# GELU moved from the state space groups to the gate, and a second set of attention buffers, in a one-layer hybrid encoder step

## The chip, the cores and the metric

One core of one Trainium2 chip runs the whole step. The metric is the device time of one execution in microseconds (us), as the median of several runs. Engines are named as the profile names them: PE is TensorE's matmul side and PEld its weight loads, DVE is VectorE, ACT is ScalarE, POOL is GpSimd, SP is SyncE, which issues the DMAs.

## The reference

One layer is computed for 2048 prompt positions and 32 sample positions, width 1024, everything in float32:

```python
h = rmsnorm(x, ln1_g) * (1 + sc1) + sh1
q, k, v, u = split(h @ w_in)                        # 8 heads, 2 kv heads, 32 groups of 16 channels
attn = sink_attention(rope(norm(q)), rope(norm(k)), v)   # own chunk of 64 and the 128 before it
ssm_y, h_last = s5(u, ...)                          # scan over positions, 64 complex states a group
g = gelu(ssm_y)
ssm_o = g * sigmoid(g @ ssm_glu_w + ssm_glu_b)
merged = concat(rmsnorm(attn), rmsnorm(ssm_o))
x = x + g1 * (merged @ w_out)
h2 = rmsnorm(x, ln2_g) * (1 + sc2) + sh2
x = x + g2 * ((silu(h2 @ w_gate) * (h2 @ w_up)) @ w_down)
```

GELU is taken element by element, so it may be applied where `ssm_y` is made or anywhere between there and its first use in `g @ ssm_glu_w` and `g * sigmoid(...)`.

## The kernel before

Tokens are handled in 17 tiles: 16 of 128 prompt positions and one of the 32 sample positions. They are taken in the order of `TILES`, prompt tiles 8 to 15, then 0 to 7, then the sample tile. "The k-th tile" below counts in that order from 0, so the 8th is prompt tile 0. Every float32 product is made of three matmuls of a high and a low half (`mm3`, L117), and nearly every operand is first split in two: ACT rounds the high half, DVE or POOL subtracts to get the low half (L101, L89).

There are four stages, all in one function:

- Stage A (to about 355 us): modulation vectors, input projection, matrices of the state space layer. The q, k, v columns of prompt tiles 0 to 5 are put off (`LATE`).
- Stage B (about 355 to 555 us): the 32 state space groups (`ssm_group`, L950), the projections put off (`deferred`, L841), and the first attention tiles (`attention_tile`, L1097). A group transposes its inputs, makes two products `v1` and `v2`, scans them on DVE, adds up `y` in PSUM, and ACT writes `t` from it with GELU (L992). `t` goes to DRAM (`gt_d`).
- Stage C (about 555 to 960 us): the remaining attention tiles, the gate (`c_prep`, L1288), the norms (`c_norm`, L1335) and the output projection (`c_out`, L1366). `c_prep` takes units of 256 tokens in the order 4, 5, 6, 7, 0, 1, 2, 3 and the sample as unit 8. Two units share one loaded buffer `gr` of 512 tokens (`g_load`, L1273): it is loaded by four DMAs when the second unit of the pair before is done, and there is only one such buffer. A unit splits `gr` into `gh` and `gl`, multiplies by `glh` and `gll` (the GLU weights) into `cb`, takes a Tanh on ACT (L1321) and multiplies by `gr` on DVE.
- Stage F (from about 962 us): gate, up and down projections, PE-bound, with SiLU on ACT.

An attention tile splits q, k and v, transposes them, and then has two halves of queries `o` = 0 and 1. For each half it makes scores `s` (8 matmuls) and calls `softmax` (L1046): DVE takes maxima into `st`, ACT takes four Exp from `s` into the buffer `pbuf` of that half with running sums, DVE finishes the sums, POOL scales `pbuf`. Then `p_split` (L1063) transposes `pbuf` on PE into `pt` and splits that into `th` and `tl`, and `p_values` (L1076) multiplies with the values into `ob` and copies to `att`. There is one `pbuf` for each half, shared by all tiles:

```python
    pe_ = [pb_.tile([128, 4, 256], F32, name=f"pbuf{o}") for o in range(2)]
```

The flows are Python generators that a class `Flow` steps in turn; attention runs as

```python
    fa = Flow(attention_tile, NT, 2, 5)
```

at most 2 tiles at a time, a new one when the last has made 5 steps, and at most `NATT` = 6 tiles ahead of the output projection. What order the instructions of one engine finally have is decided by a scheduler when the kernel is built (L1897), so a change in one flow moves instructions of the others too. Within an engine the order is then fixed: an instruction whose input is late holds up all that stand behind it.

Between stages B and C the weights `glh`, `gll` (`glu_steps`, L1180) and the eight `woh`, `wol` of the output projection (`wo_steps`, L1167) are loaded and split. The pool that holds the GLU weights and the first four `woh` is opened when the one of the projections put off (`qin`, L1199) is closed.

Of the kernel before, what the change touches and what calls it, by code (L numbers as in the profile page):

```python
# [10 lines left out]
F32 = mybir.dt.float32  # L11
F32R = mybir.dt.float32r
I32 = mybir.dt.int32
AF = mybir.ActivationFunctionType
# [9 lines left out]
NT = NPT + 1  # L24
# [13 lines left out]
NSC = DEC // LC  # L38
# [35 lines left out]
def hybrid_kernel(  # L74
# [10 lines left out]
    V, A, P, PE, SP = nc.vector, nc.scalar, nc.gpsimd, nc.tensor, nc.sync  # L85
# [14 lines left out]
    def act(out, a, func=AF.Copy, **kw):  # L100
        A.activation(out, a, func, **kw)  # L101

    def f(a):
        return a.bitcast(F32)
# [811 lines left out]
    pb_ = bin_.enter_context(tc.tile_pool(name="pb", bufs=1, reuse_waits="tile", side="right"))  # L916
# [30 lines left out]
    def part(t, dt=F32R):  # L947
        return pss.tile([128, XC], dt, tag=t, name=t)

    def ssm_group(g):  # L950
        b_, gi_ = divmod(g, GB)
        us, uss = bt_[b_]
        sm = pss.tile([128, SM], F32R, tag="sm", name="sm", bufs=SMB)
        SP.dma_start(f(sm), sm_d[g])
        ec = pss.tile([128, 2, XC], F32, tag="ec", name="ec", bufs=SMB)
        for h in range(2):
            SP.dma_start(ec[64 * h:64 * h + 64], e_d[g])
        Th, Tl = sm[:, 0:128], sm[:, 128:256]
        M1, M2 = f(sm[:, 256:384]), f(sm[:, 384:512])
        up = mbank([128, XC], nm="up")  # L960
        yield 1
        for b in range(2):
            PE.transpose(up[:, 128 * b:128 * b + 128], us[:, b, gi_].rearrange("c l h -> c (l h)"), ident)
        PE.transpose(up[:, 256:262], uss[:, gi_].rearrange("c l h -> c (l h)"), ident[0:6, 0:6])
        uh, ul = part("uh"), part("ul")
        split(uh, ul, up, A, V)
        yield 1
        v1 = mbank([128, XC], nm="v1", tag="v1", bufs=1)
        v2 = mbank([128, XC], nm="v2", tag="v2", bufs=1)
        mm3(v1, sm[:, 512:640], sm[:, 704:832], uh, ul, True, True)  # L970
        mm3(v2, sm[:, 576:704], sm[:, 768:896], uh, ul, True, True)
        w = part("w", F32)
        t = part("t", F32)
        tt(V, w[:, 1:XC], v1[:, 0:XC - 1], ec[:, 0, 1:XC], MULT)
        tt(V, t[:, 1:XC], v2[:, 0:XC - 1], ec[:, 1, 1:XC], MULT)
        tt(P, w[:, 1:XC], w[:, 1:XC], t[:, 1:XC], ADD)
        P.tensor_copy(w[:, 0:258:257], zh[:, g])
        V.tensor_tensor_scan(w[:, 1:257], r8[:, g:g + 1].to_broadcast([128, 256]), w[:, 1:257], 0.0, op0=MULT, op1=ADD)
        V.tensor_tensor_scan(w[:, 258:262], r8[:, g:g + 1].to_broadcast([128, 4]), w[:, 258:262],
                             zh[:, g, 1:2], op0=MULT, op1=ADD)  # L980
        yield 1
        for i, (e, xf) in enumerate(((P, xf1), (P if g % 2 else V, xf2))):
            x = w if i else t
            tt(e, x, w, ec[:, i], MULT)
            P.tensor_copy(xf[:, :, g], x[:, 256:262:5])
        yield 1
        y = mbank([128, XC], nm="y", tag="y", bufs=YB)
        mm3(y, Th, Tl, uh, ul, True, False)
        mm(y, M1, t, False, False)
        mm(y, M2, w, False, True)  # L990
        g2 = t
        act(g2, y, AF.Gelu_apprx_tanh)  # L992
        yield 1
        SP.dma_start(gt_d[16 * g:16 * g + 16].rearrange("h l c -> l h c"), g2[:, 0:256])
        P.tensor_copy(gsm[:, :, g], g2[:, 257:261])
        yield 1
# [26 lines left out]
    ts(V, nsink, nsink, -1.0)  # L1023
    ts(V, nsinks, nsinks, -1.0)

    pe_ = [pb_.tile([128, 4, 256], F32, name=f"pbuf{o}") for o in range(2)]
    P.memset(pe_[0][:, :, 192:256], 0.0)
    P.memset(pe_[1][:, :, 0:64], 0.0)

    def kv_split(kf, vf, dst, n):  # L1030

# [63 lines left out]
    atts = {}  # L1095

    def attention_tile(j):  # L1097
        j = TILES[j]
        n = 128 if j < NPT else DEC
        qkv = pb2.tile([128, QKV], F32, tag="qkv", name="qkv", bufs=1)  # L1100
        SP.dma_start(qkv[0:n], qkv_d[j * 128:j * 128 + n])
        yield 1
        qs = pb2.tile([128, NH, 128], F32R, tag="qs", name="qs", bufs=1)
        qv = qkv[0:n, 0:512].rearrange("p (h d) -> p h d", d=HD)
        split(qs[0:n, :, 0:64], qs[0:n, :, 64:128], qv, A, P)
        qt = pb2.tile([128, NH * 128], F32R, tag="qt", name="qt", bufs=1)
        qw = n // 2 if j < NPT else n
        qtv = qt[:, 0:NH * n].rearrange("p (o h q) -> p h o q", h=NH, q=qw)
        for hb in range(2):
            qb = bbank([128, 4, 128], F32R, nm="qb")  # L1110
            for i in range(4):
                PE.transpose(qb[:, i, 0:n], qs[0:n, hb * 4 + i], identr[0:n, 0:n])
            cp(V if hb else A, qtv[:, hb * 4:hb * 4 + 4], f(qb[:, :, 0:n]).rearrange("p h (o q) -> p h o q", q=qw))
        kf = qkv[0:n, 512:640].rearrange("p (h d) -> p h d", d=HD)
        vf = qkv[0:n, 640:768].rearrange("p (h d) -> p h d", d=HD)
        kt = pb2.tile([128, 4, 256], F32R, tag="kt", name="kt")
        att = pat.tile([128, 4, 128], F32, tag="att", name="att", bufs=NATT)
        atts[j] = att
        if j < NPT:
            vcur = kv_split(kf, vf, kt[:, :, 128:256], n)  # L1120
            if j == TILES[0]:
                pkv = pb2.tile([128, 2, 128], F32, tag="ckv", name="pkv", bufs=1)
                SP.dma_start(pkv, qkv_d[(j - 1) * 128:j * 128, 512:768].rearrange("t (a d) -> t a d", a=2))
                vprev[0] = kv_split(pkv[:, 0].rearrange("p (h d) -> p h d", d=HD),
                                    pkv[:, 1].rearrange("p (h d) -> p h d", d=HD), kt[:, :, 0:128], 128)
            elif j:
                V.tensor_copy(kt[:, :, 0:128], f(vprev[1][:, :, 128:256]))
            vpt = [vprev[0], vcur]
            vprev[0], vprev[1] = vcur, kt
            yield 1  # L1130
            vlist = [(vpt[0], 128), (vcur, 128)]
            kbs = (0, 1) if j else (1,)
            for o in range(2):
                lo, hi = (64 * o, 192 + 64 * o) if j else (128, 192 + 64 * o)
                sp = [bbank([128, 2, 256], nm="s") for _ in range(2)]
                for pr in range(4):
                    for x in range(2):
                        mm(sp[pr // 2][:, pr % 2, lo:hi], qt[:, 512 * o + 128 * pr:512 * o + 128 * pr + 128],
                           kt[:, (pr // 2) * 2 + x, lo:hi], x == 0, x == 1)
                softmax(sp, pe_[o], lo, hi, nsink)  # L1140
                yield 1
            for o in range(2):
                parts = []
                for kv in range(2):
                    parts.append(p_split(pe_[o], kbs, 2, kv))
                    yield 1
                p_values(parts, vlist, kbs, 2, att[:, :, 64 * o:64 * o + 64])
        else:
            ckv = pb2.tile([128, 2, 128], F32, tag="ckv", name="ckv", bufs=1)
            SP.dma_start(ckv[:, 0], cache_k[0, 0].rearrange("t h d -> t (h d)"))  # L1150
            SP.dma_start(ckv[:, 1], cache_v[0, 0].rearrange("t h d -> t (h d)"))
            vc = kv_split(ckv[:, 0].rearrange("p (h d) -> p h d", d=HD), ckv[:, 1].rearrange("p (h d) -> p h d", d=HD),
                          kt[:, :, 0:128], 128)
            vo = kv_split(kf, vf, kt[:, :, 128:160], n)
            sp = bbank([128, 2, 256], nm="s")
            for kv in range(2):
                for x in range(2):
                    mm(sp[:, kv, 0:160], qt[:, 128 * kv:128 * kv + 128], kt[:, kv * 2 + x, 0:160], x == 0, x == 1)
            P.memset(pe_[0][:, 0:2, 160:192], 0.0)
            softmax([sp], pe_[0], 0, 160, nsinks)  # L1160
            yield 1
            parts = [p_split(pe_[0], (0, 1), 1, kv) for kv in range(2)]
            yield 1
            p_values(parts, [(vc, 128), (vo, DEC)], (0, 1), 1, att[:, :, 0:DEC])
        yield 1
# [23 lines left out]
    def stage(nm):  # L1189
        return pw1.tile([128, 512], F32, tag="tc", name=nm, bufs=TC)  # L1190

    fa = Flow(attention_tile, NT, 2, 5)
    n = 0
    while fd.next < fd.n or fd.live:
        for fl, st, lim in ((fm, FM, G), (fd, FDS, G), (fa, FAS, NATT)):
# [75 lines left out]
    graw, ssm = {}, {}  # L1271
# [16 lines left out]
    def c_prep(u):  # L1288

        u = UNITS[u]  # L1290
        b, h = divmod(u, 2)
        if u == UNITS[0]:
            g_load(b)
        n = 256 if u < 8 else DEC
        nch = n // LC
        g = graw[b][:, :, :, nch * h:nch * h + nch].rearrange("p k l c -> p k c l")
# [14 lines left out]
        for i in range(2):  # L1311
# [3 lines left out]
            for m in range(2):  # L1315
                o = 256 * i + 128 * m
# [495 lines left out]
    for n, (L, u, p) in enumerate(steps):  # L1812
# [19 lines left out]
        b = PRODUCTS[p][2]  # L1832
# [68 lines left out]
```

## Time and profile before

| what | value |
|---|---|
| median of 3 runs | 2361.86 us (2360.06 to 2366.63) |
| profiled execution, its own time | 2357.34 us |
| its span, first to last instruction | 2355.6 us |
| mean granted clock of PE | 0.967 |
| PE, PEld busy | 94%, 87% of the span |
| DVE, POOL, ACT busy | 76%, 56%, 53% |
| DMA queue of the kernel | 52.8% of 16 engines' span |

The span is the time from the first to the last instruction on the core, and the busy time of an engine is the time with an instruction running on it. The profile also gives the clock that PE was granted in each stretch: 1.0 stands for the full 2.4 GHz, 0.5 for 1.2 GHz, and what lies between is a mean of stretches at either. A view of waits says which engine sat idle and what ended it; a view by lines groups instructions with their durations; a view of windows gives the busy time and the clock in chosen stretches.

### The profile page before, as it was taken

How to read it: one execution, taken by the hardware profiler on the slowest of the kernel's cores; microseconds unless marked ns; L12 is line 12 of the kernel's file. 1: busy time of each engine (PE TensorE's matmuls, PEld its weight loads, DVE VectorE, ACT ScalarE, POOL GpSimd, SP SyncE). 2: the span in 40 equal slices, each digit the busy share in tenths (PEclk: the TensorE clock that was granted, in tenths of full speed). 3: DMA queues.
4: the chain of work that ended last, by engine and by line, in shares of the span. 5: the costliest groups of instructions: out<-in, count | busy, mean ns of one | idle time of the engine just before them, and what ended most of it. 6: DMA issues, size and time to landing. Idle time of an engine off the chain costs nothing. (4 is left out here: it accounts for less than half of the span.)

```text
span 2355.6 us, 39042 instructions
## 1 busy us (share of the span) xinstructions
PE 2213.2 (94%) x13286; PEld 2055.3 (87%) x13286; DVE 1784.8 (76%) x2715; ACT 1252.0 (53%) x2538; POOL 1324.1 (56%) x1193
## 2 busy tenths in 40 slices
PE   7888998998989999899999998999999989999998
PEld 4576776787788878899999998999999989999998
DVE  6978876777777774766768889666678897777887
ACT  5655534556556555544445575444455744444663
POOL 1277775785656555578884246565522465655233
PEclk8899998998999999999999999999999999999999
DMA  7757767875312215567666545543365445433653
GB/s 232 265 169 235 204 201 221 252 229 170 92 57 77 78 42 172 159 188 225 199 182 216 168 138 168 158 128 107 97 200 171 126 141 157 135 103 120 193 159 122
DMA packets 429572, 380.12 MB, mean 161 GB/s; under 512 B 57326, under 2 KB 358986, under 8 KB 429372
## 3 DMA queue, kind: packets, MB, share of 16 engines
q1 hardware_dynamic: 429372, 377.63, 52.8%
q8 instruction: 104, 1.70, 0.3%
q14 instruction: 96, 0.79, 0.1%
HBM read 284.63 MB, written 92.91 MB: 160 GB/s over the span
## 5 line engine op out<-in xcount | busy, mean ns | idle before, releaser
L89 DVE TENSOR_TENSOR wl<-wr,wh 128x512 fp32r<-128x512 f32 (+1 forms) x708 | 721.0, 1036 | 226.6 <-ACT wh L101 223.7
L101 ACT ACTIVATE wh<-wr 128x512 fp32r<-128x512 f32 (+1 forms) x708 | 430.4, 616 | 532.4 <-PE fx L117 291.4
L117 PE MATMUL fx<-bh,wh 128*128 128x352 f32 (+1 forms) x1576 | 509.6, 323 | 8.4 <-DVE acc L98 4.7
L117 PE MATMUL fx<-bl,wh 128*128 128x352 f32 (+1 forms) x1576 | 508.8, 323 | 3.1 <-DVE bl L89 3.1
L117 PE MATMUL fx<-bh,wl 128*128 128x352 f32 (+1 forms) x1576 | 509.2, 323 | 0.0
L89 POOL TENSOR_TENSOR wr<-wr 128x512 f32<-128x512 f32 x256 | 379.7, 1493 | 199.1 <-DVE wl L89 158.8
L117 PEld LDWEIGHTS fx<-bh,wh 128*128 128x128 f32 x1576 | 299.6, 190 | 10.2 <-DVE acc L98 5.2
L117 PEld LDWEIGHTS fx<-bl,wh 128*128 128x128 f32 x1576 | 299.4, 190 | 3.9 <-DVE bl L89 3.9
L117 PEld LDWEIGHTS fx<-bh,wl 128*128 128x128 f32 x1576 | 299.2, 190 | 0.1
L117 PE MATMUL fy<-bh,wh 128*128 128x352 f32 (+1 forms) x792 | 254.5, 321 | 0.0
L117 PE MATMUL fy<-bh,wl 128*128 128x352 f32 (+1 forms) x792 | 254.2, 321 | 0.0
L117 PE MATMUL fy<-bl,wh 128*128 128x352 f32 (+1 forms) x792 | 254.0, 321 | 0.0
L89 POOL TENSOR_TENSOR c<-c 128x352 f32<-128x352 f32 (+1 forms) x96 | 138.4, 1442 | 135.1 <-ACT wh L101 100.6
L89 POOL TENSOR_TENSOR c<-c,acc 128x352 f32<-128x352 f32 (+1 forms) x72 | 84.7, 1181 | 171.8 <-ACT c L101 168.4
L89 POOL TENSOR_TENSOR q<-q,q 128x1408 f32<-128x1408 f32 (+3 forms) x23 | 84.6, 3682 | 123.6 <-DVE q L89 87.3
L89 DVE TENSOR_TENSOR bl<-q,bh 128x1408 fp32r<-128x1408 f32 (+3 forms) x85 | 149.8, 1765 | 5.1 <-ACT bh L101 5.1
L117 PEld LDWEIGHTS fy<-bh,wh 128*128 128x128 f32 x792 | 149.4, 189 | 0.0
L117 PEld LDWEIGHTS fy<-bl,wh 128*128 128x128 f32 x792 | 149.3, 189 | 0.0
L117 PEld LDWEIGHTS fy<-bh,wl 128*128 128x128 f32 x792 | 149.0, 188 | 0.1
L117 PE MATMUL fz<-bh,wl 128*128 128x352 f32 (+1 forms) x412 | 134.8, 328 | 9.1 <-DVE wl L89 9.1
L117 PE MATMUL fz<-bl,wh 128*128 128x352 f32 (+1 forms) x412 | 133.8, 325 | 3.8 <-DVE bl L89 3.8
L101 ACT ACTIVATE bh<-q 128x1408 fp32r<-128x1408 f32 (+3 forms) x85 | 108.9, 1286 | 51.4 <-DVE q L89 34.2
(388 smaller groups left out, 5225.4 us busy)
## 6 DMA issues: line engine op xcount, KB each, us to landing
wr<-in_w_gate_dram SPq DMA_DIRECT2D x132, 256.0 KB
wr<-in_w_up_dram SPq DMA_DIRECT2D x132, 256.0 KB
wr<-sd_d SPq DMA_DIRECT2D x96, 256.0 KB
wr<-in_w_down_dram SPq DMA_DIRECT2D x72, 256.0 KB
adw<-in_w_ada_dram SPq DMA_DIRECT2D x64, 256.0 KB
f_d<-c SPq DMA_DIRECT2D x88, 176.0 KB
sm<-sm_d SPq DMA_DIRECT2D x32, 448.0 KB
q<-f_d SPq DMA_DIRECT2D x16, 704.0 KB
```

The source lines that it names most:

```text
L89: e.tensor_tensor(out, a, b, op=op)
L101: A.activation(out, a, func, **kw)
L117: PE.matmul(out, lhsT, rhs, start=start, stop=stop, skip_group_check=more)
```

## The change

GELU is taken out of the copy that ends a state space group. The copy stays, as a plain one. `c_prep` applies GELU in place to the loaded `gr`, for two units (512 tokens) in one ACT instruction, in front of the first unit of each pair, and once for the sample. Attention gets two sets of `pbuf`, used by even and odd tiles, up to 3 tiles at a time, and some steps in `attention_tile` are placed differently. The first gate/up unit of stage F is as it was.

```diff
@@ ssm_group
-        act(g2, y, AF.Gelu_apprx_tanh)
+        act(g2, y)
@@ ahead of the attention
-    pe_ = [pb_.tile([128, 4, 256], F32, name=f"pbuf{o}") for o in range(2)]
-    P.memset(pe_[0][:, :, 192:256], 0.0)
-    P.memset(pe_[1][:, :, 0:64], 0.0)
+    pes = [[pb_.tile([128, 4, 256], F32, name=f"pbuf{i}{o}") for o in range(2)] for i in range(2)]
+    for pe_ in pes:
+        P.memset(pe_[0][:, :, 192:256], 0.0)
+        P.memset(pe_[1][:, :, 0:64], 0.0)
@@ attention_tile
+        pe_ = pes[j % 2]
         j = TILES[j]
...
                 softmax(sp, pe_[o], lo, hi, nsink)
                 yield 1
+            yield 1
             for o in range(2):
                 parts = []
                 for kv in range(2):
                     parts.append(p_split(pe_[o], kbs, 2, kv))
+                    yield 1
+                if o:
                     yield 1
                 p_values(parts, vlist, kbs, 2, att[:, :, 64 * o:64 * o + 64])
...
-    fa = Flow(attention_tile, NT, 2, 5)
+    fa = Flow(attention_tile, NT, 3, 5)
@@ c_prep
+        if u == 8 or not h:
+            x = graw[b][:, :, :, 0:64 if u < 8 else NSC]
+            act(x, x, AF.Gelu_apprx_tanh)
```

The order of the instructions moves with it. PE's order is the same up to the start of stage B and again from early in stage F on. Three places show what moves.

PE in stage C, around the 8th attention tile (`s` scores, `pt` transposes of `pbuf`, `ob` values, `co` output projection). Before:

```order
L117 MATMUL s<-kt,qt 128x128 x4
L117 MATMUL ob<-th,vs 128x256 x2
L117 MATMUL s<-kt,qt 128x128 x4
L117 MATMUL ob<-tl,vs 128x256
L117 MATMUL ob<-th,vs 128x256 x2
L117 MATMUL ob<-tl,vs 128x256
L117 MATMUL co<-woh_6918,ml 128x512
L117 MATMUL co<-woh_6919,mh 128x512
L117 MATMUL co<-wol_6923,mh 128x512
L117 MATMUL co<-woh_6919,ml 128x512
L1069 MATMUL pt<-cpk,pbuf_4093 128x128 x2
```

The same tile now, `pbuf_4096` being a buffer of the tile before it:

```order
L117 MATMUL co<-woh_6923,ml 128x512
L117 MATMUL s<-kt,qt 128x64 x8
L1070 MATMUL pt<-cpk,pbuf_4096 128x128 x4
L117 MATMUL s<-kt,qt 128x128 x4
L117 MATMUL co<-woh_6835,ah 128x512
L117 MATMUL co<-wol_6839,ah 128x512
L117 MATMUL co<-woh_6835,al 128x512
L117 MATMUL s<-kt,qt 128x128 x4
L117 MATMUL co<-woh_6836,ah 128x512
L117 MATMUL co<-wol_6840,ah 128x512
L117 MATMUL co<-woh_6836,al 128x512
```

Before, the tile's first scores (8 more, just ahead of the rows shown) and its first `pt` had 12 `ob`, 8 `s` and 4 `co` between them. Now it is 4 `pt`, 8 `s`, 24 `co`, 2 small matmuls `rb` and 12 `ob`; the scores stand ahead of the last transposes of the tile before.

ACT at the end of stage B (`t<-y` ends a state space group). Before, from the last group on:

```order
L101 ACTIVATE t<-y 128x262
L101 ACTIVATE vs<-qkv 128x2x128
L101 ACTIVATE att<-ob 64x4x64
L101 ACT_TABLE_LOAD
L101 ACTIVATE pbuf_4094,st<-s,st 128x192 x4
L101 ACTIVATE st<-st 128x4
L101 ACTIVATE th<-pt 128x512
L101 ACTIVATE ah<-att 128x512 x2
L101 ACTIVATE th<-pt 128x512
L101 ACTIVATE glh<-gf 128x512 x4
L101 ACTIVATE att<-ob 64x4x64
```

And now, where four of the groups' copies are still to come:

```order
L101 ACTIVATE glh<-gf 128x512 x4
L101 ACTIVATE th<-pt 128x512
L101 ACTIVATE woh_6835<-wf,vecs 128x512 x2
L101 ACTIVATE t<-y 128x262
L101 ACTIVATE woh_6836<-wf,vecs 128x512 x2
L101 ACTIVATE t<-y 128x262
L101 ACTIVATE woh_6837<-wf,vecs 128x512 x2
L101 ACTIVATE t<-y 128x262
L101 ACTIVATE woh_6838<-wf,vecs 128x512 x2
```

The splits of the GLU weights and of the first four `woh` have moved ahead of the last groups.

ACT in stage C around the third GELU, now:

```order
L101 ACTIVATE t,rso<-xc 128x512
L101 ACTIVATE ah<-att 128x512
L101 ACT_TABLE_LOAD
L101 ACTIVATE gr<-gr 128x2048
L101 ACTIVATE t<-co,rso 128x512
L101 ACT_TABLE_LOAD
L101 ACTIVATE pbuf_4093,st<-s,st 128x192 x4
L101 ACTIVATE st<-st 128x4
L101 ACTIVATE th<-pt 128x512
L101 ACTIVATE gh<-gr 128x512 x2
```

GELU and two table loads stand in front of a tile's Exp. Of 20 table loads in the program before, 11 are left: one at the start, nine around the five GELUs, one for SiLU.

## Rows read from the trace of the kernel before

**Rows 1.** The page, part 1: busy time of each engine.

```profile
PE 2213.2 (94%) x13286; PEld 2055.3 (87%) x13286; DVE 1784.8 (76%) x2715; ACT 1252.0 (53%) x2538; POOL 1324.1 (56%) x1193
```

**Rows 2.** Windows: stretch, its length; busy and (count) by engine; PEclk; DMA; GB/s.

```profile
355.00:385.00 30.00, 21.39 (x113) 17.88 (x111) 14.62 (x30) 13.39 (x37) 14.58 (x16) 0.77 0.89 259
385.00:550.00 165.00, 151.88 (x983) 132.60 (x983) 126.86 (x280) 85.98 (x200) 130.69 (x252) 1.00 0.71 216
550.00:602.00 52.00, 37.77 (x200) 30.54 (x199) 41.51 (x69) 37.95 (x88) 19.88 (x16) 0.77 0.54 169
...
672.00:692.00 20.00, 13.55 (x80) 11.96 (x78) 16.12 (x29) 9.97 (x36) 10.26 (x11) 0.76 0.13 46
724.00:740.00 16.00, 11.45 (x62) 10.14 (x61) 11.17 (x24) 7.84 (x26) 10.14 (x9) 0.80 0.18 65
776.00:792.00 16.00, 13.44 (x75) 10.81 (x74) 12.23 (x24) 8.59 (x31) 11.47 (x11) 1.00 0.28 92
824.00:842.00 18.00, 13.14 (x74) 11.80 (x73) 13.02 (x27) 10.29 (x32) 11.32 (x11) 0.81 0.10 35
966.00:2356.00 1390.00, 1356.65 (x8550) 1346.28 (x8548) 1068.57 (x1231) 722.76 (x1319) 750.77 (x495) 0.99 0.52 156
```

**Rows 3.** Timeline of PE, 680 to 692 and two later stalls: start, us, what, [idle before].

```profile
681.18 0.39 PE L117 MATMUL ob<-tl,vs 128*128 128x256 f32 x1 [2.01 <-DVE tl L89]
...
687.46 0.69 PE L1069 MATMUL pt<-cpk,pbuf 128*128 128x128 f32 x2 [4.44 <-DVE st L89]
...
735.52 1.11 PE L1069 MATMUL pt<-cpk,pbuf 128*128 128x128 f32 x4 [4.55 <-POOL pbuf L89]
...
834.69 1.11 PE L1069 MATMUL pt<-cpk,pbuf 128*128 128x128 f32 x4 [4.86 <-POOL pbuf L89]
```

**Rows 4.** Timeline of PE: starts of two neighbouring co and two neighbouring cb.

```profile
583.29 0.28 PE L117 MATMUL cb<-gl,glh 128*128 128x256 f32 x1
583.41 0.28 PE L117 MATMUL cb<-gh,gll 128*128 128x256 f32 x1
...
727.19 0.39 PE L117 MATMUL co<-woh,al 128*128 128x512 f32 x1
727.42 0.39 PE L117 MATMUL co<-woh,ah 128*128 128x512 f32 x1
```

**Rows 5.** Timeline of PE, DVE and ACT at the hand-over from stage B to C.

```profile
560.88 1.94 PE L1069 MATMUL pt<-cpk,pbuf 128*128 128x128 f32 x8 [3.45 <-ACT pbuf L101]
...
565.32 2.52 DVE L89 TENSOR_TENSOR gll<-gf,glh 128x512 fp32r<-128x512 f32 x4
568.06 2.55 ACT L101 ACTIVATE woh<-wf,vecs 128x512 fp32r<-128x512 f32 x4
571.51 1.12 ACT L101 ACTIVATE gh<-gr 128x512 fp32r<-128x512 f32 x1
588.92 0.50 PE L117 MATMUL co<-woh,mh 128*128 128x512 f32 x1 [2.65 <-ACT mh L101]
591.29 0.79 PE L117 MATMUL co<-wol,mh 128*128 128x512 f32 x1 [1.86 <-DVE wol L98]
```

**Rows 6.** Groups by line of ACT, 355 to 560: count, busy us, mean ns, idle before.

```profile
L101 ACT ACT_TABLE_LOAD x18 | 23.1, 1283 | 10.0 <-PE y L117 7.4 <-DVE st L89 2.4
L101 ACT ACTIVATE us<-ur 128x1024 f32<-128x1024 f32 x8 | 8.5, 1060 | 14.7 <-DMA ur<-u_d 14.7
```

**Rows 7.** Timeline of ACT around one switch of the table.

```profile
420.53 0.39 ACT L101 ACTIVATE uh<-up 128x262 fp32r<-128x262 f32 x1 [1.86 <-PE y L117]
420.94 1.28 ACT L101 ACT_TABLE_LOAD   x1
422.23 0.42 ACT L101 ACTIVATE pbuf<-s,st 128x192 f32<-128x192 f32 x1
```

**Rows 8.** Waits: PE on ACT (385 to 550), ACT on DMA (whole span).

```profile
PE y L117 <- ACT t L101: 4.3, 5, 1.2
ACT gh L101 <- DMA gr<-gt_d: 10.0, 5, 4.1
```

## Prediction

> **What bounds the kernel now.** I read the page first: PE is busy 94% of the span, its weight loads 87%, and no other engine is above 76% [rows 1]. So PE is the bound, and the change takes no product away. It can only win back time that PE loses. For that I read the windows next: in a stretch, PE loses about its length less its busy time times the granted clock (an estimate, since the clock is a mean). Stage F, 966 to 2356, loses 1390 - 1356.65 x 0.99 = 47 us of 1390 [rows 2], and its order on PE stays. The losses that the change can reach are in three places:
>
> - the start of stage B, 355 to 385: 30 - 21.39 x 0.77 = 13.5 us; and the rest of B, 385 to 550: 165 - 151.88 = 13.1 us [rows 2]
> - the hand-over from B to C, 550 to 602: 52 - 37.77 x 0.77 = 22.9 us [rows 2]
> - four stalls inside C, about 50 us apart: 9.7, 6.8, 2.6 and 7.4 us, 26.5 together [rows 2]
>
> For the stalls I looked at PE's timeline. In three of the four, PE stands 4.44, 4.55 and 4.86 us in front of `pt`, the transposes of the softmax result [rows 3]; the first has 2.01 us more a little earlier. In those windows the granted clock is 0.76 to 0.81, while the one of 776 to 792, with only short waits, keeps 1.00 [rows 2]: a stall of over 4 us is followed by a piece at 1.2 GHz and costs about half as much again (9.7 us lost for 6.45 us of idling in the first).
>
> **Stalls in C.** They belong to the 8th, 10th, 12th and 14th tile, each the first of a pair. One pair of `pbuf` serves all tiles, so a tile's Exp cannot start before the `pt` of the tile before are through. The distance on PE between a tile's first scores and its first `pt` is the cover for its softmax. For the 8th tile it was 12 `ob`, 8 `s` and 4 `co`: with 0.23 us from one `co` to the next and 0.12 for `cb` or `ob` (both 256 columns) [rows 4], and about 0.09 for an `s` (estimated by columns), 1.4 + 0.7 + 0.9 = 3.0 us. With 6.45 us of waits the softmax needed about 9.5. Now the cover is 24 `co`, 12 `ob`, 8 `s`, 4 `pt` and 2 `rb`: 5.5 + 1.4 + 0.7 + 0.5 + 0.4 = 8.5 us, one us short. Counted in the same way over the order, the 10th goes from 7.6 to 12.1 us where 7.6 + 4.55 = 12.2 was needed, the 14th from 7.6 to 10.4 where 12.5 was needed, the 12th from 10.3 to 10.9. That leaves 1 + 0 + 2 + 2 us or so, too short each to cost clock going by 776 to 792. But the need is no constant: it contains DVE's queue. I count 8.5 of 26.5 us as staying: **-18**. Bounds: all gone, -26.5; or -4, if DVE alone sets the end.
>
> **Hand-over.** The splits of four `glh` and eight of the sixteen `woh` move ahead of the last state space groups. They cost ACT 4 x 0.6 + 8 x 0.64 = 7.5 us (2.55 for four `woh`), DVE 2.52 for the four `gll` and about 8 x 0.7 for the `wol` [rows 5]; they then lie beside the groups' matmuls, where DVE has 38 of 165 us free and ACT 79 [rows 2]. After 555 DVE had no room: PE waited 1.86 us for `wol`, 2.65 for `mh`, and 3.45 for a softmax of the 4th tile [rows 5]. That tile's cover grows from 4.5 to 6.5 us. The first two waits lose their cause or most of it, the third shrinks; with the clock I take **-9** of 22.9. Bounds -15 and -3.
>
> **GELU, taken out.** A copy from PSUM lasts as long as GELU did, so the 32 copies cost nothing new. What goes is the switching of ACT's table in stage B, 18 loads of 1.283 us [rows 6]. ACT is far from full there, so it counts only where PE waited behind it: PE waited 4.3 us for `t` in the main part of B [rows 8]. I take -3 for that, and -3 for the start of B, where 24 `kp` of ready projection work now stand in front of the transposes that waited for loaded inputs: **-6**, bounds -10 and 0. The Trainium skill's page ScalarE: Activation LUTs, section What ACT_TABLE_LOAD costs, gives 1.28 us for a load and about 1.38 for a drain, 2.66 for a switch. Here the load starts 0.02 us after the instruction in front ends, and the Exp 0.01 us after the load [rows 7]: 1.3 us a switch, and the drain does not show. By the page a GELU with two loads would hold ACT 2.7 us longer than I reckon below.
>
> **GELU, put in.** One instruction of 2048 elements, twice the longest plain ACT operation on rows: 1024 take 1.06 us [rows 6], so 2048 lie between 1.06 and 2.12; I take 2.0, nearest to twice. With a load on each side ACT is held 4.6 us, four times, and less for the sample. What stands behind it on ACT: the Exp of a tile, which PE's `pt` wait for through DVE and POOL. Each GELU also waits for `gr`, as `gh` did before (10.0 us in 5 waits [rows 8]), and now the Exp stand behind that wait. At the hand-over nothing hides it: load, GELU and then `gh`, which started at 571.51 [rows 5], so +3.3 for the first GLU products (the second load comes behind), unless the earlier weights let `gr` arrive sooner. I take **+3**, bounds 0 and +5. At the other three boundaries the cover of the tile is 10 us or more; I take 1.5 each and 0.5 for the sample: **+5**, bounds 0 and +14.
>
> Added work elsewhere: two more memsets on POOL at the start of B, beside PE work, and no DMA is added; moved DMAs (weights earlier, `gr` behind fewer of them on SP) gain within the hand-over's term. Stage F starts earlier and is otherwise unchanged: 0.
>
> **Sum**: -18 - 9 - 6 + 3 + 5 = -25 us against the profiled execution of 2357.34. That lies 4.5 below the median of the runs, 2361.86; set on the median, 2337. The bounds give 2361.9 - 51.5 = 2310 and 2361.9 - 7 + 19 = 2374. A difference of 0.3%, 7 us, is about what a measurement of this kernel can tell from no change.
>
> **Rivals.**
>
> *The stalls are DVE's* (0.13). In the first stall PE's wait ended with `st` on DVE [rows 3], and the other two end on POOL, which works after DVE: the buffers may not be what is late. Then a second set only shifts the stall: -4 in place of -18, sum -11, 2351. Against it: the cover on PE grows whatever DVE does.
>
> *GELU takes back what is won* (0.09). Each of the three GELUs inside C holds ACT 4.6 us and waits some 2 us for `gr` (10.0 in 5 [rows 8]) with a softmax behind: 6.6 x 3 = 20 and 8 at the hand-over against -33, sum -5, 2357: no change to be told. This is what the Trainium skill's rule would make of it (ScalarE: Activation LUTs, section Table sets: the hidden batching unit: group the calls by table set), as Tanh and Exp in stage C needed no switch and GELU breaks into them; the trace agrees so far, as of 20 loads 18 lie in B [rows 6].
>
> *Slower* (0.08). The same place, with the stalls kept because DVE sets them (-4) and no room in the cover: every GELU then appears on PE in full, and with the clock falling at half as much again, 4.6 x 1.5 = 6.9, three times, 21; the hand-over comes out 6 worse for the first GLU products waiting behind the load and GELU at 1.2 GHz; stage B gives 2. Sum -4 + 21 + 6 - 2 = +21, 2383. It decides itself on the cover: where a tile needs 12.2 us, as the 10th did, and 4.6 more, a cover under 17 us stalls in full. For it: covers of 8.5 to 12 us. Against it: not every GELU meets a tile that is so late, since ACT is idle 45% of C's time.
>
> *The forecast*: 0.70.
>
> **Numbers.** The likeliest is 2337. Its own bounds with the first rival and the second's time reach from 2315 to 2358; this leaves out the slower rival, part of the second, and the far ends. Faster by over 0.3% (below 2355): 0.79, from the forecast nearly whole and most of the first rival. Within: 0.12. Slower: 0.09.
>
> **What would show it.** Right: the waits of `pt` for `pbuf` and `st` in C fall from over 4 us to under 2, the clock near the old stalls stays at 1.00, `wol` and `mh` no longer stop PE near 590, 11 table loads in all, a GELU near 2.0 us, stage F as long as before (about 1390 us), C shorter by 20 us or so and B by 6. Wrong: stalls of 4 us with a clock near 0.8 at the tiles behind a GELU; or `pt` waits of the old size with DVE's `st` late; or a first GLU product that comes later after the last `y` than it did.

## Result and the profile after

| | before | changed |
|---|---|---|
| median of 4 runs, us | 2362.66 (2360.06 to 2366.63) | 2348.16 (2347.37 to 2350.29) |
| ratio to before | 1 | 0.9933, 95% interval 0.9920 to 0.9946 |
| profiled execution, span | 2357.34, 2355.6 | 2348.45, 2346.6 |

The change makes the kernel 14.5 us faster by the medians; 25 were forecast, and the time lies inside the range. The profiled execution of before lies 5.3 us below its median, that of the changed kernel on its own median, so the two traces show 9 us of the 14.5. One execution of e1 below (6064.53 us) and one of e4 (2663.02 us) took far longer than all others; they are left out of every median and ratio.

The page of the changed kernel, part 1 [rows 1]: PE has as many products as before.

```profile
PE 2206.6 (94%) x13286; PEld 2047.7 (87%) x13286; DVE 1778.6 (76%) x2715; ACT 1247.2 (53%) x2534; POOL 1322.7 (56%) x1195
```

Windows of the changed kernel, the stretches of [rows 2] and one more, 602 to 672 (columns as there):

```profile
355.00:385.00 30.00, 17.39 (x95) 14.04 (x93) 11.72 (x21) 8.67 (x17) 12.36 (x18) 0.83 0.92 275
385.00:550.00 165.00, 154.58 (x986) 136.34 (x986) 122.85 (x281) 69.94 (x202) 129.14 (x234) 0.96 0.70 215
550.00:602.00 52.00, 35.01 (x190) 29.32 (x190) 41.52 (x75) 37.84 (x87) 20.36 (x31) 0.80 0.54 169
602.00:672.00 70.00, 65.19 (x395) 57.21 (x396) 46.42 (x79) 39.37 (x99) 42.36 (x39) 0.95 0.24 72
672.00:692.00 20.00, 18.34 (x115) 15.97 (x114) 19.36 (x27) 10.04 (x25) 12.59 (x10) 1.00 0.14 47
...
724.00:740.00 16.00, 14.50 (x86) 12.00 (x85) 13.62 (x24) 14.25 (x33) 8.80 (x7) 1.00 0.29 82
...
776.00:792.00 16.00, 15.70 (x103) 13.90 (x103) 11.87 (x27) 9.89 (x33) 11.32 (x11) 1.00 0.22 75
...
824.00:842.00 18.00, 17.52 (x122) 15.66 (x120) 11.02 (x23) 14.48 (x40) 9.99 (x12) 1.00 0.17 59
```

The last four rows are the places of the old stalls. PE loses 1.7, 1.5, 0.3 and 0.5 us there, 4.0 where it lost 26.5, and the granted clock stays at 1.00. The rows above them give some of it back: 355 to 385 loses 15.6 us (13.5 before), 385 to 550 16.6 (13.1), 550 to 602 24.0 (22.9). The row of before that goes with 602 to 672 is this one:

```profile
602.00:672.00 70.00, 68.94 (x433) 61.22 (x433) 50.82 (x83) 37.95 (x100) 45.18 (x40) 1.00 0.26 80
```

There the loss goes from 70 - 68.94 = 1.1 us to 70 - 65.19 x 0.95 = 8.1.

At the start of stage B the longest wait of PE is a new one, for the inputs `us` that a state space group transposes (waits, 345 to 386: us in total, times, longest; in before it is 0.8 us):

```profile
PE up L963 <- ACT us L101: 7.0, 2, 6.7
```

The hand-over is late as a whole. The view by tile of `y` (count, shortest, median and longest ns, first and last start) gives for before:

```profile
L117 PE MATMUL y<-uh,sm x64: 277/285/392, 386.5 to 551.1; 128*128 128x262 f32 x64
```

and for the changed kernel:

```profile
L117 PE MATMUL y<-uh,sm x64: 278/287/585, 386.6 to 565.5; 128*128 128x262 f32 x64
```

The last group ends 14 us later, and `gt_d`, `gr` and the GLU products hang on it: the first of these products starts 23.0 us after the last `y`, and did so 22.3 us after it before. The timeline of the changed kernel on ACT, from 557 us:

```profile
557.77 1.34 ACT L101 ACTIVATE woh<-wf,vecs 128x512 fp32r<-128x512 f32 x2
559.00 0.40 ACT L101 ACTIVATE t<-y 128x262 f32<-128x262 f32 x1
...
579.92 1.28 ACT L101 ACT_TABLE_LOAD   x1 [2.15 <-DMA gr<-gt_d]
581.21 1.91 ACT L101 ACTIVATE gr<-gr 128x2048 f32<-128x2048 f32 x1
583.03 0.71 ACT L101 ACTIVATE woh<-wf,vecs 128x512 fp32r<-128x512 f32 x1
583.75 1.28 ACT L101 ACT_TABLE_LOAD   x1
585.05 0.42 ACT L101 ACTIVATE pbuf<-s,st 128x192 f32<-128x192 f32 x1
...
587.35 2.08 ACT L101 ACTIVATE gh<-gr 128x512 fp32r<-128x512 f32 x2
```

and on PE, with the waits from 545 to 610:

```profile
552.83 1.12 PE L117 MATMUL y<-t,sm 128*128 128x262 f32 x2 [2.26 <-POOL t L89]
...
559.45 0.39 PE L117 MATMUL y<-uh,sm 128*128 128x262 f32 x1 [2.52 <-ACT t L101]
...
586.01 1.11 PE L1070 MATMUL pt<-cpk,pbuf 128*128 128x128 f32 x4 [4.60 <-ACT pbuf L101]
...
590.90 0.58 PE L117 MATMUL cb<-gl,glh 128*128 128x256 f32 x1 [1.61 <-DVE gl L89]
602.26 0.50 PE L117 MATMUL co<-woh,mh 128*128 128x512 f32 x1 [1.99 <-ACT mh L101]
606.09 0.80 PE L117 MATMUL co<-woh,ml 128*128 128x512 f32 x1 [3.09 <-DVE ml L89]
```

ACT waits 2.15 us for `gr`, is held 1.28 + 1.91 + 1.28 us by the loads and GELU, with one `woh` among them, and only then comes the Exp for which PE waits 4.60 us. Waits of `y` as long as those at 552 and 559 are new too (the longest for `t` on ACT was 1.2 us before [rows 8]); at the second, two of the weights' splits stand on ACT just before the copy `t` for which PE waits.

To compare kernels whose stages end at different times, the table below adds up, in pieces of 5 us, length minus PE's busy time times its granted clock, from 300 us on: to 385, to the last `y`, over the 60 us behind it, and from there to the first product of stage F. All are estimates, in us, from the one profiled execution of each.

| kernel | last y | F starts | to 385 | B to last y | 60 us behind it | rest of C | sum |
|---|---|---|---|---|---|---|---|
| before | 551.1 | 955.4 | 16.7 | 13.6 | 23.0 | 34.2 | 87.6 |
| changed | 565.5 | 947.9 | 19.0 | 24.7 | 21.2 | 15.0 | 79.8 |
| changed again (e9) | 561.7 | 943.8 | 17.7 | 22.1 | 21.5 | 13.1 | 74.6 |
| e1 GELU move alone | 550.1 | 954.9 | 15.8 | 13.4 | 26.9 | 31.0 | 87.2 |
| e2 attention alone | 580.6 | 948.9 | 16.8 | 38.4 | 13.9 | 7.8 | 76.9 |
| e3 no GELU | 563.5 | 931.2 | 18.2 | 23.3 | 13.1 | 8.4 | 62.9 |
| e4 one set | 546.5 | 932.7 | 16.1 | 13.7 | 23.6 | 11.6 | 65.1 |
| e10 one set again | 549.5 | 935.2 | 19.0 | 14.3 | 23.6 | 11.2 | 68.1 |
| e5 old steps | 544.1 | 951.7 | 18.6 | 6.9 | 28.6 | 30.8 | 84.8 |
| e6 second set unused | 567.8 | 954.1 | 18.1 | 25.2 | 23.5 | 16.1 | 83.0 |
| e7 second set behind | 559.0 | 946.1 | 17.7 | 21.0 | 23.6 | 14.1 | 76.4 |
| e8 one set, GELU in groups | 556.8 | 941.5 | 16.4 | 22.0 | 22.8 | 12.6 | 73.8 |
| e11 two tiles | 544.0 | 933.2 | 15.4 | 10.2 | 25.5 | 17.8 | 68.9 |
| e12 one set, no GELU | 546.5 | 930.8 | 17.1 | 12.0 | 22.5 | 12.5 | 64.1 |

Two programs stand in it twice, the changed kernel with 79.8 and 74.6 and the one of e4 with 65.1 and 68.1. So a difference of about 5 us in the sum tells nothing. The executions traced are not all typical: those of e6, e7 and e8 lie 3.6 to 4.7 us above the medians of their kernels, that of e11 11.7 us below.

### The profile page after: what moved, and what is told of

Read it like the earlier page. It is cut to its first block, busy times and chain, and to the rows that moved or that the text cites. A ratio compares the mean times of both kernels' runs of the same rounds, so it can differ in the third digit from the quotient of the medians.

```text
span 2346.6 us, 39039 instructions
## 1 busy us (share of the span) xinstructions
PE 2206.6 (94%) x13286; PEld 2047.7 (87%) x13286; DVE 1778.6 (76%) x2715; ACT 1247.2 (53%) x2534; POOL 1322.7 (56%) x1195
## 5 line engine op out<-in xcount | busy, mean ns | idle before, releaser
L117 PEld LDWEIGHTS fx<-bh,wh 128*128 128x128 f32 x1576 | 298.2, 189 | 10.1 <-DVE acc L98 5.2
```

Of the source, the lines that this page charges most:

```text
L117: PE.matmul(out, lhsT, rhs, start=start, stop=stop, skip_group_check=more)
```

## The experiments

Four kernels at a time ran on one chip, beside the kernel before: e1 to e4, e5 to e8, e9 to e12. The median of before was 2363.92, 2366.24 and 2365.42 us there; kernels of different groups are compared by their ratios to it.

### The two halves of the change apart

e1: the changed `ssm_group` and `c_prep`, attention as before.

> GELU moved to the gate, attention as before (one set of pbuf, two tiles at a time, old steps). Theory 1 (the gain is the attention's; GELU at the gate costs time at the hand-over): the three waits of PE in front of pt near 687, 735 and 834 us of the span stay at 4 to 5 us, the hand-over is some 5 us worse, the start and main part of stage B no shorter: 2363 to 2370, slower than before or the same. Theory 2 (the 18 table loads taken out of stage B are what was won): stage B shorter by 5 us or more, 2352 to 2357.

e2: the changed attention, GELU as before.

```diff
-        act(g2, y)
+        act(g2, y, AF.Gelu_apprx_tanh)
...
-        if u == 8 or not h:
-            x = graw[b][:, :, :, 0:64 if u < 8 else NSC]
-            act(x, x, AF.Gelu_apprx_tanh)
```

> Attention changed (two sets of pbuf, three tiles at a time, new steps), GELU left in the state space groups (26 table loads in the program instead of 11). Theory 1: the three waits of over 4 us in stage C are gone as in the changed kernel, and the hand-over has no GELU in front of a tile's Exp: 2338 to 2344, faster than the changed kernel by 4 to 10 us. Theory 2: the table loads stay in stage B, so most of the gain is gone: 2354 to 2360.

Measured: e1 2354.39 us, 0.9963 (0.9948 to 0.9978); e2 2349.15 us, 0.9938 (0.9921 to 0.9955). Neither time is theory 1's: e1's is that of theory 2, and e2's lies between the two. The place of the gain is theory 1's all the same. The waits of PE from 680 to 955 us in e1 (us in total, times, longest), which in before are 10.1 and 4.4:

```profile
PE pt L1069 <- POOL pbuf L89: 10.4, 5, 4.1
PE pt L1069 <- DVE st L89: 4.2, 1, 4.2
```

and the same view of e2:

```profile
PE pt L1070 <- POOL pbuf L89: 0.7, 2, 0.4
```

So stage C's gain is the attention's alone. Where e1 wins its 9.5 us by the medians is not seen: its traced execution is 3.4 us shorter than that of before, 3.0 of it in stage F with its order unchanged, the last `y` comes 1.0 us sooner, not 5, and the sums of the table differ by 0.4. In e2 stage B loses 38.4 us instead of 13.6. From 385 us to the last group PE waits 8.8 us there for `t` on ACT (4.8 before, 4.5 in the changed kernel), which is a part of it, and there are 25 table loads from 355 to 970 us; what makes up the rest is not shown (groups by line of ACT; count, busy us, mean ns, idle before):

```profile
L101 ACT ACT_TABLE_LOAD x25 | 32.1, 1283 | 16.9 <-DVE st L89 12.2 <-issue 3.0 <-PE y L117 1.4
```

Moving GELU on top of e2 takes 13.7 us out of B (38.4 to 24.7) and puts 7.3 into the hand-over and 7.2 into the rest of C: in time, nothing (0.9938 to 0.9933).

### What GELU costs at the gate

e3: the changed kernel with GELU left out altogether, so that neither the state space outputs nor what follows from them are the reference's.

> The changed kernel with GELU left out of the gate, so no GELU is computed anywhere: the price of the five GELU and their table loads. Theory 1: the wait of 4.6 us of PE in front of pt at the hand-over goes, and the first GLU products come 3 to 5 us sooner after the last y: 5 to 9 us less than the changed kernel, 2339 to 2343. Rival (the GELU at the gate are hidden behind other work of ACT): within 2 us of the changed kernel, 2346 to 2350.

Measured: 2332.9 us, 0.9875 (0.9854 to 0.9896). The price is (0.9933 - 0.9875) x 2364 = 13.7 us, by the two intervals some 8 to 20. So it is above theory 1's 5 to 9, though not clear of the 9; the rival (hidden) falls. In the table the hand-over goes from 21.2 to 13.1 us and the rest of C from 15.0 to 8.4. PE's order differs only in part from the changed kernel's and is that of e2.

### Buffers, steps, or the third tile

e4: one set of `pbuf`, all else as changed.

```diff
-    pes = [[pb_.tile([128, 4, 256], F32, name=f"pbuf{i}{o}") for o in range(2)] for i in range(2)]
+    pes = [[pb_.tile([128, 4, 256], F32, name=f"pbuf{i}{o}") for o in range(2)] for i in range(1)]
...
-        pe_ = pes[j % 2]
+        pe_ = pes[0]
```

> The changed kernel with a single set of pbuf, three tiles at a time and the new steps kept. Theory 1a (the second set is what removes the stalls): a tile's Exp wait for the transposes of the tile before again, waits of 3 to 5 us in front of pt in stage C come back, 2358 to 2365. Theory 1b (the order of the steps alone removes them, the set is not needed): waits under 2 us, 2346 to 2352.

e5: both sets and three tiles, the steps of before.

```diff
                 yield 1
-            yield 1
             for o in range(2):
...
                     yield 1
-                if o:
-                    yield 1
```

> The changed kernel with the steps of attention_tile as before; two sets of pbuf, three tiles at a time and GELU at the gate stay. By the order on PE the cover of the 8th, 10th, 12th and 14th tile (first scores to first pt) is 3.0, 7.6, 7.6 and 7.6 us, as before or shorter. Theory 2a (the steps make the cover, and the cover removes the stalls): waits in front of pt of 4 us or so come back in stage C, some 20 us more lost there than in the changed kernel: 2360 to 2370. Theory 2b (the second set or the third tile removes them): waits under 2 us, 2345 to 2352.

Measured: e4 2337.18 us, 0.9896 (0.9874 to 0.9919), faster than the changed kernel, which neither expectation had. e5 2355.62 us, 0.9961 (0.9945 to 0.9976), 4 us below what theory 2a gave, as stage B loses only 6.9 us, but with the stalls back. (Its interval just touches the changed kernel's.) Waits of PE in e5, 680 to 955 us:

```profile
PE pt L1070 <- POOL pbuf L89: 9.4, 6, 3.3
PE pt L1070 <- DVE st L89: 4.6, 1, 4.6
```

and in the changed kernel, where `st` is gone from the list for `pt`:

```profile
PE pt L1070 <- POOL pbuf L89: 1.7, 2, 1.4
```

The cover, in us, counted over PE's order with the spacings of [rows 4], goes with it:

| tile | before | changed | e4 one set | e5 old steps | e11 two tiles |
|---|---|---|---|---|---|
| 8th | 3.0 | 8.4 | 7.7 | 3.0 | 5.1 |
| 10th | 7.6 | 12.1 | 10.4 | 7.6 | 8.9 |
| 12th | 10.3 | 10.9 | 12.3 | 7.6 | 9.1 |
| 14th | 7.6 | 10.4 | 10.4 | 7.6 | 7.2 |
| rest of C, loss | 34.2 | 15.0 | 11.6 | 30.8 | 17.8 |

One set with the new steps has the long cover and no wait of `pt` over 1.8 us; two sets with the old steps have the short cover and the stalls. So the steps take the stalls away, and the second set does nothing for it.

How the steps do it is shown in part. For the 8th tile it is the cover. ACT waits for DVE's `st` in front of that tile's Exp, in before and in the changed kernel, nearly as long in both, but now PE has 8.4 us of other work meanwhile instead of 3.0 (ACT's timeline, before first):

```profile
683.54 0.31 ACT L101 ACTIVATE pbuf<-s,st 128x64 f32<-128x64 f32 x1 [6.91 <-DVE st L89]
```

```profile
690.63 0.32 ACT L101 ACTIVATE pbuf<-s,st 128x64 f32<-128x64 f32 x1 [6.14 <-DVE st L89]
```

For the 10th and the 14th the steps change one thing more. GELU stands on ACT ahead of these tiles' Exp, and in e5 it waits for `gr` there, in the changed kernel hardly; in before `gh` stands there and waits 2.2 and 3.7 us for `gr`. ACT's timeline in e5, then in the changed kernel:

```profile
724.77 1.28 ACT L101 ACT_TABLE_LOAD   x1 [3.41 <-DMA gr<-gt_d]
...
824.00 1.28 ACT L101 ACT_TABLE_LOAD   x1 [2.90 <-DMA gr<-gt_d]
```

```profile
725.56 1.28 ACT L101 ACT_TABLE_LOAD   x1 [0.30 <-DMA gr<-gt_d]
...
820.26 1.28 ACT L101 ACT_TABLE_LOAD   x1
```

No run separates this from the cover for these two tiles, and e11 below has a 14th tile whose cover is 7.2 us and whose `pt` waits less than 1 us.

e11: one set, and two tiles at a time, `Flow(attention_tile, NT, 2, 5)`.

> One set of pbuf, new steps, GELU at the gate, but two tiles at a time instead of three. By the order on PE the covers of the 8th, 10th, 12th and 14th tile are 5.1, 8.9, 9.1 and 7.2 us (with three at a time 7.7, 10.4, 12.3 and 10.4; before 3.0, 7.6, 10.3 and 7.6). Theory 5a (cover decides, and a third tile is needed for it): waits of 2 to 4 us in front of pt come back in part, 2343 to 2352. Theory 5b (the new steps alone suffice): 2335 to 2341.

Measured: 2352.5 us, 0.9930 (0.9905 to 0.9955). Its profiled execution (2340.78) was the fastest of six, the others 2347 to 2355, so the trace doesn't show where most of them lose their time. The time is 0.5 us above theory 5a's range; in the one execution traced the big stalls are away, as 5b has it, and `pt` waits 2.5 us for POOL. From e1 this kernel differs in the steps alone, and the rest of C loses 17.8 us where e1 loses 31.0, though the intervals of the two ratios meet. Whether stage C needs the third tile stays open.

### Why two sets are slower than one

e6: the second set stays allocated, but is neither cleared nor used.

```diff
-    for pe_ in pes:
+    for pe_ in pes[0:1]:
...
-        pe_ = pes[j % 2]
+        pe_ = pes[0]
```

> The changed kernel with the second set of pbuf allocated in its place but neither cleared nor used: all tiles share the first set. PE's order is that of the changed kernel. Theory 3a (the second set costs stage B its 11 us by its room alone: it pushes the first tile's qkv buffer onto memory that a late tile of stage A still holds, so its load is issued near 370 us instead of 355, and the order of stage B is another): 2345 to 2351, stage B as long as in the changed kernel. Theory 3b (the cost comes from clearing or using the second set): 2335 to 2341, as with one set.

e7: the second set in a pool of its own behind `pb2`, the pool of `qkv`.

```diff
     pb2 = bin_.enter_context(tc.tile_pool(name="pb2", bufs=2, reuse_waits="tile", side="right"))
+    pb3 = bin_.enter_context(tc.tile_pool(name="pb3", bufs=1, reuse_waits="tile", side="right"))
...
-    pes = [[pb_.tile([128, 4, 256], F32, name=f"pbuf{i}{o}") for o in range(2)] for i in range(2)]
+    pes = [[(pb3 if i else pb_).tile([128, 4, 256], F32, name=f"pbuf{i}{o}") for o in range(2)] for i in range(2)]
```

> The changed kernel with the second set of pbuf in a pool of its own behind the pool of qkv, so that qkv lies where it lay before; both sets are used. Theory 3a (room): qkv is loaded near 355 us, stage B loses some 14 us instead of 25, 2334 to 2342. Theory 3b (use of the second set lets attention run ahead of the state space groups and costs them): the last y stays near 565 us, 2345 to 2351.

e9 and e10: the changed kernel and e4 once more, on one chip.

> The changed kernel once more, beside the next three on one chip: 0.992 to 0.995 of the time before, as measured (0.9933), and the measure for the next run.

> The kernel with one set of pbuf, new steps, three tiles and GELU at the gate, once more beside the changed kernel. Theory 3a (the second set costs room in stage B and gives nothing in stage C): 8 to 14 us less than the changed kernel on the same chip, 0.987 to 0.991 of the time before. Rival (the first look at it was a favourable chip): within 3 us of the changed kernel.

Measured: e6 2352.26 us, 0.9946 (0.9927 to 0.9964); e7 2344.68 us, 0.9912 (0.9890 to 0.9934); e9 2351.57 us, 0.9940 (0.9917 to 0.9963); e10 2340.58 us, 0.9889 (0.9868 to 0.9910). Runs of e9 (2349.28 to 2355.64) and e10 (2337.20 to 2344.24) don't meet: the second set costs 11.0 us with GELU at the gate, as theory 3a had it. (With GELU in the groups, e2 and, further on, e8 differ by 0.0061, 14 us, and their intervals don't meet; without GELU, e3 and e12 differ by 0.0026 with intervals that overlap.) e6 lies 1 us above theory 3a's range; it is as slow as the changed kernel by ratio, its loss in B is as large (25.2), and PE's order is the same but for the numbers of the buffers. So, with the new steps, the cost is that of the room, 8 KB in each partition, and not of clearing or use.

What room does is seen first in the loads of `qkv`. By tile (first start), before:

```profile
L1101 SPq DMA_DIRECT2D qkv<-qkv_d x3: 430/437/597, 355.6 to 386.5; - x3
```

then the changed kernel, e6 and e7:

```profile
L1103 SPq DMA_DIRECT2D qkv<-qkv_d x3: 319/327/448, 370.6 to 389.1; - x3
```

```profile
L1103 SPq DMA_DIRECT2D qkv<-qkv_d x3: 320/327/592, 374.6 to 392.6; - x3
```

```profile
L1104 SPq DMA_DIRECT2D qkv<-qkv_d x4: 320/382/437, 357.2 to 399.2; - x4
```

The timeline of SP in the changed kernel shows the first of them behind the last stores from `qkvo`, a buffer of stage A; before, it was ahead of them:

```profile
366.93 0.65 SPq L812 DMA_DIRECT2D qkv_d<-qkvo  x1
367.62 0.42 SPq L815 DMA_DIRECT2D out_dram<-qkvo  x1
...
370.59 0.45 SPq L1103 DMA_DIRECT2D qkv<-qkv_d  x1
```

With the second set behind `pb2` the load is back at 357 us, and e7 is faster than e6 on the same chip by 7.6 us (a few of their runs overlap), but its time lies between the two theories, its last `y` comes at 559, and B still loses 21.0 us, now with waits for `sm`, a load of each group, that come to 2.1 us in before and 0.6 in the changed kernel (PE's waits, 340 to 570 us):

```profile
PE v L117 <- DMA sm<-sm_d: 8.2, 4, 3.7
```

And e5, with the late load (369.3 us) but the old steps, loses the least of all in B (6.9). So room matters by what order it leads to together with the steps. One sign of it is PE's wait for `us` at the start of B: the longest is 3.1 to 6.7 us in all seven traces with the second set, used or not, and at most 0.9 us in the seven with one set. But up to 385 us the changed kernel loses only 2.3 us more than before, so how the rest of the 11 us comes about stays open, as does whether `qkv` lies on the memory of `qkvo`: that fits its place in the queue, but no run shows the addresses.

### GELU with one set

e8: e4 with GELU left in the groups; e12: e4 with no GELU at all (outputs as in e3), in PE's order of e8.

> One set of pbuf, three tiles at a time, new steps, and GELU left in the state space groups (18 table loads in the program). Theory 4a (the move of GELU is worth nothing in sum: what it takes from the hand-over and stage C it gives back in stage B): 2335 to 2341, as with GELU at the gate. Theory 4b (GELU at the gate costs some 14 us in stage C that B does not give back, as B has one tile less in it here): 2325 to 2333.

> One set of pbuf, three tiles, new steps, and GELU left out of the kernel altogether: its price in the state space groups, as PE's order is that of the kernel with one set and GELU in the groups. Theory 4a (GELU costs stage B about what it costs at the gate, some 10 to 15 us): 2322 to 2328. Theory 4b (in the groups it is hidden): within 3 us of that kernel, 2333 to 2340.

Measured: e8 2336.89 us, 0.9877 (0.9855 to 0.9899); e12 2331.52 us, 0.9849 (0.9828 to 0.9871). e8 is as theory 4a had it, e12 lies between the two. On the chip of e10, GELU at the gate costs 2340.58 - 2331.52 = 9.1 us with one set; the 13.7 with two are too uncertain to call that less. In the groups it costs (0.9877 - 0.9849) x 2366 = 6.6 us by ratios whose intervals overlap; its loss in B is 22.0 against 12.0. The two places can't be told apart in time. e8 and e4 (with e10) are the fastest kernels here that compute the whole step, 25 to 29 us below before by the medians.

## Why the prediction was right, and where its sum was wrong

The forecast (faster by well over 0.3%, time within the range) held; the sum had -25 where -14.5 was measured. The direction came from the place that was named, the stalls of stage C. That the time fell inside the range owes something to the width of the range, 43 us, and to luck: 2348.2 lies 11 us above the likeliest 2337 and nearer to the first rival's 2351, and errors of some 19 us in stage B and 7 in the price of GELU were in part made good by stage C, which without GELU (e3) gained 25.8 us in the table where 18 were forecast. The terms, against the losses of the traces:

- **Stalls in C, -18**: -22.5 by the windows, so the size was nearly right. That the steps remove them is shown by e5 and e4 from both sides; the cover as the reason is shown for the 8th tile, and for the 10th and 14th it stands beside the wait for `gr` on ACT. The step "one pair of `pbuf` serves all tiles, so a tile's Exp cannot start before" was wrong as a reason: with one pair and the new steps the stalls are gone as well, and what the 8th tile's Exp waits for in before is DVE's `st`.
- **Hand-over, -9**: in its place it is there. Without GELU (e3) the 60 us behind the last `y` lose 13.1 where before lost 23.0, -9.9. But the weights' splits that moved ahead of the last groups took part in making these late: B to the last `y` went from 13.6 to 23.3. Both together are 36.6 before and 36.4 in e3. I had laid the splits beside the groups' matmuls at no price, on ACT's 79 idle us out of 165; what counts is that a copy `t`, for which PE waits, can stand behind them (2.52 us at 559). Of the waits that were to go near 590, the one for `wol` is gone, but `mh` still stops PE for 1.99 us, and `ml` now for 3.09.
- **GELU, taken out, -6**: before to e1 the table shows -1.1 up to the last `y` (30.3 to 29.2), so in the trace the 18 loads were as good as hidden with the old steps. Of the 3 us for the start of B nothing came: 355 to 385 loses 2 us more, and PE waits 6.7 us for the inputs `us`, the wait that the projection work was to cover. With the new steps the same removal is worth more, 11.5 us (e2 to the changed kernel, 55.2 to 43.7), and is given back at the gate.
- **GELU, put in, +3 and +5**: the instruction was sized well, 1.91 us for an estimate of 2.0, and the switch is 1.3 us, as [rows 7] had it. By the Trainium skill's page ScalarE: Activation LUTs (section What ACT_TABLE_LOAD costs) 1.4 us of drain would come on top of each load. Here GELU starts 0.01 us after its load and the Exp 0.02 us after the second. The price at the hand-over was 8.1 us, not 3: I wrote that the second load comes behind the GLU's `gh`, but the Exp of a tile stands between GELU and `gh`, and PE's `pt` waits 4.60 us for it; the wait for `gr`, late with the last `y`, is in front of all. In the rest of C it was 6.6 for my 5.
- **Added work elsewhere, 0**: this is the step that failed. I priced the second set by its two memsets, and not by the 8 KB that shift what lies behind it. With the new steps that costs 11.0 us; up to the last `y` the kernel loses 43.7 us where before lost 30.3. The gain of 6 forecast for B was not there to be lost: with one set it is 29.8 and 33.3 (e4, e10).
- **The rivals**: that the stalls are DVE's was right in what is late (`st`, and not the buffers) and falls in what it forecast, since with DVE's `st` as late as before the cover takes the stall away. GELU taking back what is won came true by about half: 13.7 of its 28. The rule of the Trainium skill's page ScalarE: Activation LUTs, section Table sets: the hidden batching unit, is to batch calls by table set. Here the switches fell from 26 in e2 to 11 in the changed kernel and from 18 in e8 to 11 in e4, and neither time changed by more than the intervals; the switch to Exp at the hand-over stands ahead of an Exp that PE waits 4.60 us for.

## What to carry to other kernels

Count the instructions between a producer and its consumer in the bottleneck engine's final order: this cover told here that the stalls would shrink, where the number of buffers did not matter; then look at what else stands ahead of the producer on its own engine. Price a buffer by its room as well, by leaving it allocated and unused: here a later load was issued 15 to 19 us later for it, and the order of a whole stage changed. A table switch costs what waits behind it, so fewer switches at a worse place were no gain here.

## What the runs showed that was not expected

- 8 KB per partition that no instruction touches cost (0.9946 - 0.9896) x 2365 = 12 us with the new steps (e6 against e4).
- A GELU over 2048 elements took 1.91 us, less than two copies of 1024 at 1.06 each [rows 6].
- Executions of one program spread by more than the traces' differences suggest: before ran from 2355.02 to 2370.81 us in 15 runs on one chip, so a trace of one execution can stand 5 to 10 us off its median.
